# Layer 0's banded heads: from two score passes and a product by query to one pass, a softmax by query and weights turned by TensorE

## The chip, the cores and the metric

The kernel runs on one core of one Trainium2 chip. The metric is the device time of one execution in microseconds (us), taken as the median of several runs. An execution is also profiled once; all rows below come from that profile.

## What is computed

Two blocks follow each other: a two-layer attention block and a pool-and-feed-forward block. Layer 0 has eight global heads, eight banded ("window") heads and four memory heads, each gated and then projected out. Only the banded heads change. For each of the eight heads, 1024 queries stand in 8 blocks of 128, and each block sees its own and the two neighbouring blocks of keys:

```
def window_gqa(q, k, v, sink, rel_bias):
    ...
    rel = kpos[None, :] - qpos[:, None]
    band = jnp.abs(rel) <= WINDOW          # WINDOW = 128
    bias = rel_bias[t5_bucket(rel)]
    ...
        s = jnp.einsum('bqkgd,bskd->bkgqs', qblk, kb) * scale + bias
        s = jnp.where(valid, s, -jnp.inf)
        m = jnp.maximum(jnp.max(s, axis=-1, keepdims=True), sk)
        p = jnp.exp(s - m)
        denom = jnp.sum(p, axis=-1, keepdims=True) + jnp.exp(sk - m)
        return jnp.einsum('bkgqs,bskd->bqkgd', p / denom, vb)
```

`sk` is one learned number per head (the sink): it enters the maximum and the denominator, but has no value row.

## The kernel before, in words

All products are made of float32 numbers split into a high and a low part, so that one dense product is three matmuls (lines 261, 264 and 265: high by high, high by low, low by high).

Layer 0 runs two streams at once. `att` holds the attention of 12 items (four pairs of global heads, four pairs of banded heads, four memory heads). `fill` holds the dense products of layer 0: queries, keys, gates, and six of the eight column tiles of the output projection. `weave` lets each stream advance in proportion to numbers given by hand (232 for `att`, 290 for `fill`). A scheduler of the framework then sets the final order on each engine; `att` has the higher priority there, and the first of every four products of `fill` is tied behind an earlier score product of `att` (`mark` and `paced`). Every engine works through its list in order. All loads and stores are issued from SyncE's queue, also in order.

A banded pair `i` is done in two parts.

- `win_pre` (line 918 on), run beside the item before: for each head it multiplies each query block by its two or three key blocks (line 930, scores with the query in the partition), adds the bias and takes the maximum with the sink (line 931, in one VectorE instruction and a read of its accumulator). The eight columns of negated maxima are turned into rows (`max_row`, line 481) and written by DMA into the 65th row of the tile `W`.
- `win_main` and `pair_main`: the scores are multiplied a second time with the key in the partition (lines 557 and 558; the 65th row subtracts the maximum), the bias is added (line 955), then come the exponential (469), its high part (471) and its low part (142, half of them on GpSimd). `narrow` multiplies the weights of each query block by the values with the query in the partition (lines 668 and 669; the first two of 130 value columns are constants and give the denominator), closes a group of two or three query blocks with a copy, the sink, a reciprocal and two GpSimd instructions (679 to 685), and turns the finished blocks back (691).

The tiles of scores live in a pool of three PSUM buffers (`sp`, tag `s`), two more (`op`) hold the sums of the products with the values. `wide`, which the global heads use, has the values as weights and up to 512 queries as columns (lines 616 and 617).

Of the kernel before, what the change touches and what calls it, by code (L numbers as in the profile page):

```python
# [8 lines left out]
F32 = mybir.dt.float32  # L9
# [52 lines left out]

ROLL = [[0, 1, 2], [3, 4, 5], [6, 7]]
# [79 lines left out]
class Build:  # L145
# [377 lines left out]
    def v_tiles(self):  # L523

        V = [self.ap.tile([128, 8, 130], F32R, name=f"V{i}") for i in range(2)]
        for v in V:
            self.nc.gpsimd.memset(raw(v[:, :, 0:2]), 2.0)
        return V

    def load_v(self, v, V):  # L530

        for i in range(2):
            self.dma(out=V[:, :, 2 + 64 * i:66 + 64 * i], in_=v[i])

# [42 lines left out]
    def wide(self, O, U, V, tiles, perm=False):  # L577
# [30 lines left out]
        def pv(s, i, P):  # L608
            j, a, b = tiles[i]
            for g, x0, x1 in parts[i]:  # L610
# [5 lines left out]
                mm(o, V[s][:, j, 2:130], P[0][:, x], start=new, stop=False, skip_group_check=True)  # L616
                mm(o[0:64], V[s][:, j, 2:66], P[1][:, x], start=False, stop=i == touch[g][-1], skip_group_check=True)  # L617
# [3 lines left out]
        def close(s, g):  # L621
# [5 lines left out]
            if s == 0:  # L627
                return
# [15 lines left out]

    def narrow(self, O, U, V, tiles, groups, sink):


        nc = self.nc
        mm = nc.tensor.matmul
        group = {t: g for g, ts in enumerate(groups) for t in ts}  # L650
        touch = {}
        for i, (j, a, b) in enumerate(tiles):
            for t in range(a // 128, b // 128):
                touch.setdefault(group[t], []).append(i)
        bank = {}
        T = self.po.tile([128, 8, 2, 64], F32, tag="sg", name="T")

        def pv(s, i, P):
            j, a, b = tiles[i]
            with self.tc.manual_schedule(engines={mybir.EngineType.PE}):  # L660
                for t in range(a // 128, b // 128):
                    g = group[t]
                    new = (s, g) not in bank
                    if new:
                        bank[s, g] = self.op.tile([128, 512], F32, tag="od"[g % 2], name="o")[:, 0:130 * len(groups[g])].rearrange("p (t f) -> p t f", f=130)
                    x = slice(128 * t - a, 128 * t - a + 128)
                    o = bank[s, g][:, t - groups[g][0]]
                    mm(o, P[0][:, x], V[s][:, j], start=new, stop=False, skip_group_check=True)
                    mm(o[:, 0:66], P[1][:, x], V[s][:, j, 0:66], start=False, stop=i == touch[g][-1], skip_group_check=True)  # L669
            for g, ts in enumerate(groups):  # L670
                if i == touch[g][-1]:
                    close(s, g, ts)


        def close(s, g, ts):

            o, n = bank[s, g], len(ts)
            e = self.po.tile([128, 512], F32, tag="oe", name="oe", bufs=2)[:, 0:130 * n].rearrange("p (t f) -> p t f", f=130)
            (nc.scalar.copy if g % 2 else nc.vector.tensor_copy)(e, o)
            q = slice(ts[0], ts[-1] + 1)  # L680
            nc.vector.tensor_tensor(out=e[:, :, 0], in0=e[:, :, 0], in1=sink[s][:, q], op=ALU.add)
            R = self.small.tile([128, 8], F32, tag="R", name="R")
            nc.vector.reciprocal(R[:, 0:n], e[:, :, 0])
            nc.gpsimd.tensor_tensor(out=T[:, q, s], in0=e[:, :, 2:66], in1=e[:, :, 66:130], op=ALU.add)
            nc.gpsimd.tensor_tensor(out=T[:, q, s], in0=T[:, q, s], in1=R[:, 0:n].unsqueeze(2).to_broadcast([128, n, 64]), op=ALU.mult)
# [989 lines left out]
```

## Time and profile before

| | |
|---|---|
| median of 3 runs | 2456.99 us (2454.39 to 2458.63) |
| the profiled execution's own time | 2456.56 us |
| its span, first to last instruction | 2454.8 us |
| TensorE busy in the span | 2345.8 us (96%) |
| VectorE, ScalarE, GpSimd busy | 1733.0, 1069.4, 957.8 us |
| mean granted TensorE clock | 0.977 of full speed |
| banded heads, first to last instruction of their own | 471.5 to 734.8 us |

The table is read so: TensorE has work almost all the time, but its matmuls are pipelined and their ends modelled, so that a busy TensorE can still be slower than its best. Two things take time without showing as idle: a clock below 1, and short waits hidden under the modelled ends.

### The profile page before, as it was taken

The page shows a single profiled execution, that of the slowest core. Times are in us where ns is not written, and L with a number is a line of the kernel's source. Part 1 is how long each engine was busy: PE and PEld are TensorE (multiplying, and loading weights), DVE is VectorE, ACT ScalarE, POOL GpSimd, SP SyncE. Part 2 cuts the span into 40 slices and gives each one's busy share as a digit, 9 for nine tenths or more (in the row PEclk, how much of TensorE's full clock was granted, in tenths as well). Part 3 has the DMA queues.
Part 4 walks back from the last instruction along what each step waited for, and adds up shares of the span by engine and source line. Part 5 has one row for each costly group of instructions (what it writes and reads, how often), then busy time and mean ns, then how long its engine had stood idle before and what let it go on. Part 6 is the DMA issues. An engine that isn't in the chain of part 4 may idle for free.

```text
span 2454.8 us, 33066 instructions
## 1 busy us (share of the span) xinstructions
PE 2345.8 (96%) x11238; PEld 1927.1 (79%) x11238; DVE 1733.0 (71%) x2863; ACT 1069.4 (44%) x1937; POOL 957.8 (39%) x817
## 2 busy tenths in 40 slices
PE   7989999999999999999999999989899999999999
PEld 6966776777877878878897877867578888888887
DVE  6767987777776466777886889688977464646554
ACT  5425655564453364434453446444444131323231
POOL 3117886883340144547674772475600000000000
PEclk9989999998999999999999999999899999999999
DMA  6752234234455557676766656522122111111112
GB/s 207 215 144 65 86 106 122 91 102 137 125 195 198 188 189 194 173 214 186 206 167 195 184 172 239 165 86 78 62 77 79 48 52 43 52 48 48 48 48 90
DMA packets 235393, 314.37 MB, mean 128 GB/s; under 512 B 102007, under 2 KB 120951, under 8 KB 235224
## 3 DMA queue, kind: packets, MB, share of 16 engines
q1 hardware_dynamic: 235224, 312.26, 42.0%
q8 instruction: 89, 1.46, 0.3%
q14 instruction: 80, 0.66, 0.1%
HBM read 225.02 MB, written 87.03 MB: 127 GB/s over the span
## 4 chain that ended last, share of the span: by engine, by line
PE 76%; DVE 11%; DMA 5%; issue 3%; ACT 2%; POOL 2%; SPq 1%; DVEq 0%; POOLq 0%; ACTq 0%
PE ps L261 20%; PE ps L264 20%; PE ps L265 20%; PE s L557 3%; PE s L558 2%; DVE wlo L142 2%; PE o L617 2%; PE o L616 2%; DVE pl L142 1%; PE s L867 1%; PE s L1230 1%; DVE mcg L868 1%; DMA hl<-y 1%; DVE sx L1425 1%; POOL acc L606 1%
## 5 line engine op out<-in xcount | busy, mean ns | idle before, releaser
L261 PE MATMUL ps<-hh,whi 128*128 128x512 f32 x1888 | 749.0, 399 | 19.7 <-ACT hh L415 8.2
L264 PE MATMUL ps<-hl,whi 128*128 128x512 f32 x1888 | 751.6, 398 | 9.2 <-DVE hl L416 7.5
L265 PE MATMUL ps<-hh,wlo 128*128 128x512 f32 x1888 | 753.1, 399 | 3.6 <-DVE wlo L142 2.5
L242 ACT CAST whi<-wraw 128x512 fp32r<-128x512 f32 (+1 forms) x400 | 244.8, 614 | 481.4 <-PE ps L264 387.4
L261 PEld LDWEIGHTS ps<-hh,whi 128*128 128x128 f32 x1888 | 361.3, 192 | 98.8 <-ACT hh L415 8.2
L264 PEld LDWEIGHTS ps<-hl,whi 128*128 128x128 f32 x1888 | 361.4, 191 | 87.8 <-DVE hl L416 9.2
L265 PEld LDWEIGHTS ps<-hh,wlo 128*128 128x128 f32 x1888 | 361.1, 191 | 81.1 <-DVE wlo L142 3.7
L606 POOL TENSOR_TENSOR acc<-acc,p 128x512 f32<-128x512 f32 (+2 forms) x272 | 321.7, 1190 | 238.8 <-ACT p L469 185.7
L142 DVE TENSOR_TENSOR wlo<-wraw,whi 128x512 fp32r<-128x512 f32 (+1 forms) x388 | 327.6, 848 | 63.7 <-ACT whi L242 53.5
L142 POOL TENSOR_TENSOR pl<-p,ph 128x512 fp32r<-128x512 f32 (+2 forms) x192 | 234.1, 1222 | 79.2 <-ACT ph L471 66.9
L471 ACT CAST ph<-p 128x512 fp32r<-128x512 f32 (+2 forms) x304 | 162.2, 543 | 32.5 <-PE o L669 6.7
L469 ACT ACTIVATE p<-p 128x256 f32<-128x256 f32 (+2 forms) x192 | 98.1, 515 | 163.1 <-DVE p L1257 107.3
L1497 DVE TENSOR_TENSOR xacc<-ps,xacc 128x512 f32<-128x512 f32 x96 | 66.2, 691 | 131.4 <-PE ps L265 130.9
L1469 DVE TENSOR_TENSOR hz<-ps,rbc 128x512 f32<-128x512 f32 x88 | 60.7, 690 | 116.4 <-PE ps L265 114.1
L264 PE MATMUL ps<-al,whi 128*128 128x512 f32 x352 | 139.1, 396 | 0.0
L265 PE MATMUL ps<-ah,wlo 128*128 128x512 f32 x352 | 138.7, 396 | 0.0
L261 PE MATMUL ps<-ah,whi 128*128 128x512 f32 x352 | 138.4, 396 | 0.0
L1473 ACT ACTIVATE cv<-hz,vecs 128x512 f32<-128x512 f32 x88 | 71.6, 816 | 130.9 <-DVE hz L1469 128.4
L142 DVE TENSOR_TENSOR pl<-p,ph 128x512 fp32r<-128x512 f32 (+1 forms) x112 | 104.1, 929 | 28.6 <-ACT ph L471 21.4
L617 PE MATMUL o<-pl,V 128*64 128x384 f32 (+2 forms) x288 | 95.0, 348 | 9.9 <-DVE pl L142 6.4
L469 ACT ACTIVATE p<-s 128x512 f32<-128x512 f32 x112 | 66.3, 596 | 78.3 <-PE s L558 66.4
L1257 DVE TENSOR_TENSOR p<-s,MB 128x384 f32<-128x384 f32 (+2 forms) x128 | 68.8, 550 | 40.6 <-POOL pl L142 18.5
(259 smaller groups left out, 4478.7 us busy)
## 6 DMA issues: line engine op xcount, KB each, us to landing
wraw<-in_w SPq DMA_DIRECT2D x116, 256.0 KB
wraw<-in_wfi SPq DMA_DIRECT2D x112, 256.0 KB
wraw<-in_wo SPq DMA_DIRECT2D x72, 256.0 KB
g<-evf SPq DMA_DIRECT2D x48, 256.0 KB
wraw<-in_wfo SPq DMA_DIRECT2D x40, 256.0 KB
sg<-g SPq DMA_DIRECT2D x32, 256.0 KB
y<-O SPq DMA_DIRECT2D x14, 512.0 KB
hl<-y SPq DMA_DIRECT2D x14, 512.0 KB
```

The costliest lines, as they stand in the source:

```text
L142: out_eng.tensor_tensor(out=out, in0=a, in1=b, op=ALU.subtract)
L242: nc.scalar.copy(hi, raw[:, q:q + e])
L261: i = mm(ps, wh, h, start=first, stop=False, skip_group_check=True)
L264: mm(ps, wh, l, start=False, stop=False, skip_group_check=True)
L265: mm(ps, wl, h, start=False, stop=last, skip_group_check=True)
L469: nc.scalar.activation(p, s, AF.Exp)
L471: nc.scalar.copy(ph, p)
L557: self.mark(mm(ps[:, 0:n], K0[s][0:k0, js], U[s][0:k0, a:b], start=True, stop=False))
L606: nc.gpsimd.tensor_tensor(out=t, in0=t, in1=p[:, x0 - a:x1 - a], op=ALU.add)
L617: mm(o[0:64], V[s][:, j, 2:66], P[1][:, x], start=False, stop=i == touch[g][-1], skip_group_check=True)
L1257: nc.vector.tensor_tensor(out=p, in0=ps, in1=MB[:, s, o:o + b - a], op=ALU.add)
L1473: nc.scalar.activation(t, z[:, 2:514], AF.Identity, scale=self.v("cw2", j), bias=self.v("cb", j))
```

## The change

The first score pass, the second pass by key, the row of maxima and the product by query go away. One pass is left: the queries of the banded heads are stored negated (scale -0.125), the bias tile is negated once per pair on ScalarE, and the one VectorE instruction that was the first pass now gives the minimum, which is the negated maximum, over bias and negated sink (`nsink`). The exponential takes `scale=-1` and that minimum as its bias, and sums each row on the way. For every two query blocks the sink's share is added, a reciprocal taken, and the weights are multiplied by it and by 0.5 (one block on GpSimd, the other on VectorE). Then `turn` transposes, for each key block, its two or three pieces on TensorE into one PSUM tile of the same three-buffer pool; ScalarE copies the high part, VectorE makes the low part, and `wide` multiplies with the values. The values lose their two constant columns. `half` is now marked after the first head's scores, and for the fourth pair after the second head's last turn.

```
-        V = [self.ap.tile([128, 8, 130], F32R, name=f"V{i}") for i in range(2)]
+        return [self.ap.tile([128, 8, 128], F32R, name=f"V{i}") for i in range(2)]
...
-            if s == 0:
+            if s == 0 or not sums_to:
                 return
...
+    def load_uw(self, st, q, s):
+        U = self.load_hi(q, s)
+        W = self.up.tile([128, S], F32R, tag="W", name="W", bufs=2)
+        self.dma(out=W[0:64], in_=q[1][64 * s:64 * s + 64])
+        self.nc.gpsimd.memset(raw(W[64:65, :]), 0.0)
...
+                ps = self.sp.tile([128, 512], F32, tag="s", name="s")
+                self.mark(mm(ps[:, 0:n], U[:, ts], KA[:, ks], start=True, stop=False))
+                mm(ps[:, 0:n], W[0:65, ts], KB[:, ks], start=False, stop=True)
...
+                nc.vector.tensor_tensor_reduce(out=ps[:, 0:n], in0=ps[:, 0:n], in1=TA[:, s, o:o + n], scale=1.0, scalar=self.nsink[:, h:h + 1], op0=ALU.add, op1=ALU.min, accum_out=negm[:, bb])
+                nc.scalar.activation(p[:, 0:n], ps[:, 0:n], AF.Exp, scale=-1.0, bias=negm[:, bb], accum_out=D[:, bb])
...
+            nc.scalar.activation(es[:, mm2], negm[:, mm2], AF.Exp, bias=self.sink[:, h:h + 1])
+            nc.vector.tensor_tensor(out=es[:, mm2], in0=D[:, mm2], in1=es[:, mm2], op=ALU.add)
+            nc.vector.reciprocal(R[:, mm2], es[:, mm2])
...
+                (nc.gpsimd if n2 == 0 else nc.vector).tensor_scalar(out=P[s, b][:, 0:n], in0=P[s, b][:, 0:n], scalar1=R[:, b:b + 1], scalar2=0.5, op0=ALU.mult, op1=ALU.mult)
...
+        def turn(s, j):
+            _, a, b = tiles[j]
+            t = self.sp.tile([128, 512], F32, tag="s", name="pt")
+            for q in range(a // 128, b // 128):
+                o = (j - max(q - 1, 0)) * 128
+                nc.tensor.transpose(t[:, q * 128 - a:q * 128 - a + 128], P[s, q][:, o:o + 128], self.ident)
+            ph = self.pp.tile([128, b - a], F32R, tag="ph", name="ph")
+            nc.scalar.copy(ph, t[:, 0:b - a])
+            pl = self.pp.tile([128, b - a], F32R, tag="pl", name="pl")
+            sub(nc.vector, pl, t[:, 0:b - a], raw(ph))
...
+                new = [(s, j) for j in range(8) if (j <= 2 * m or m == 3) and (m == 0 or j > 2 * m - 2)]
+                ready += new
+                yield from behind(len(new), 1)
...
-                self.drain(weave((att(), 232.0), (fill, 290.0)))
+                self.drain(weave((att(), 245.0), (fill, 290.0)))
```

How this moves instructions is shown at three places. The first is TensorE in the middle of a banded pair before the change: `o` are sums of products with the values, `ph` and `pl` the high and low part of one tile of weights, `s` scores, `ps` a dense product of `fill`.

```order
L668 MATMUL o_6139<-V0_1626,ph_6151 128x130
L669 MATMUL o_6139<-V0_1626,pl_6153 128x66
L930 MATMUL s_6250<-KA1_1633,U_6067 128x256
L668 MATMUL o_6180<-V0_1626,ph_6151 128x130
L669 MATMUL o_6180<-V0_1626,pl_6153 128x66
L261 MATMUL ps_6386<-hh_83,whi_5830 128x512
L264 MATMUL ps_6386<-hl_84,whi_5830 128x512
L668 MATMUL o_6139<-V0_1626,ph_6170 128x130
```

There a tile of weights comes straight from the exponential of its scores, and the first pass of the next pair (line 930) stands between. The same engine, in the middle of the second banded pair after the change; `pt` are tiles of turned weights, `P` the weights by query:

```order
L915 MATMUL pt_5985<-ident_58,P_5864 128x128
L915 MATMUL pt_5985<-ident_58,P_5870 128x128
L915 MATMUL pt_5985<-ident_58,P_5888 128x128
L915 MATMUL pt_6001<-ident_58,P_5870 128x128
L915 MATMUL pt_6001<-ident_58,P_5888 128x128
L915 MATMUL pt_6001<-ident_58,P_5919 128x128
L609 MATMUL o_5935<-ph_5989,V0_1628 128x256
L609 MATMUL o_6011<-ph_5989,V0_1628 128x128
L895 MATMUL s_6018<-KA0_1631,U_5824 128x256
L896 MATMUL s_6018<-KB0_1630,W_5827 128x256
L257 MATMUL ps_6137<-hh_83,whi_5906 128x512
```

The high part `ph_5989` is ScalarE's copy of `pt_5985`; its first product now stands three transposes behind the last transpose that it needs, and the next scores and the dense products are queued behind it.

The second place is the start of the second banded pair on TensorE, after the change:

```order
L895 MATMUL s_5861<-KA0_1631,U_5488 128x384
L896 MATMUL s_5861<-KB0_1630,W_5491 128x384
L895 MATMUL s_5867<-KA0_1631,U_5488 128x384
L896 MATMUL s_5867<-KB0_1630,W_5491 128x384
L915 MATMUL pt_5878<-ident_58,P_5838 128x128
L895 MATMUL s_5885<-KA0_1631,U_5488 128x384
L896 MATMUL s_5885<-KB0_1630,W_5491 128x384
L915 MATMUL pt_5878<-ident_58,P_5853 128x128
L895 MATMUL s_5916<-KA0_1631,U_5488 128x384
L896 MATMUL s_5916<-KB0_1630,W_5491 128x384
L257 MATMUL ps_6024<-hh_83,whi_5636 128x512
```

`P_5838` and `P_5853` are the weights of the first two query blocks of this pair, whose scores stand only a few rows earlier; no dense product lies between.

The third place is VectorE in the same pair. Before the change, in a banded pair's main part (`oe` is a closed group of products, `mt` the row of maxima):

```order
L955 TENSOR_TENSOR p_6352<-s_6349,TB_6056 128x384
L142 TENSOR_TENSOR pl_6307<-p_6302,ph_6305 128x256
L955 TENSOR_TENSOR p_6370<-s_6367,TB_6056 128x384
L142 TENSOR_TENSOR pl_6357<-p_6352,ph_6355 128x384
L483 CAST mt_6401<-s_6399 8x128
L679 COPY oe_6342<-o_6245 128x260
L931 ISA s_6407,mc_6406<-s_6407,TA_6064,sink_1624 128x256
```

After it, where the transposes of the first place are copied (`evl` and `wlo` belong to `fill`):

```order
L426 SCALAR_TENSOR_TENSOR evl_6095<-evf_6092,evh_6094 128x512
L138 TENSOR_TENSOR pl_5991<-pt_5985,ph_5989 128x384
L138 TENSOR_TENSOR pl_6007<-pt_6001,ph_6005 128x384
L903 TENSOR_TENSOR es0_5833<-mc_5832,es0_5833 128x2
L898 ISA s_6018,negm_6014<-s_6018,TA_5341,nsink_1626 128x256
L898 ISA negm_6014 128x1
L904 RECIPROCAL R_5834<-es0_5833 128x2
L908 TENSOR_SCALAR P_5977<-P_5977,R_5834 128x256
```

Every low part is now VectorE's, and the small instructions of the softmax stand in line between the large ones.

## Rows read from the trace of the kernel before

**Rows 1.** The page's first line.

```profile
span 2454.8 us, 33066 instructions
```

**Rows 2.** Busy time by stage: stretch, length, PE, PEld, DVE, ACT, POOL (instructions), granted clock, DMA.

```profile
541.00:735.00 194.00, 180.74 (x978) 154.69 (x976) 150.71 (x361) 97.34 (x217) 82.33 (x95) 0.93 0.49 155
735.00:926.00 191.00, 185.07 (x893) 152.18 (x892) 101.05 (x163) 80.90 (x137) 35.19 (x32) 0.99 0.59 193
140.00:541.00 401.00, 377.76 (x1580) 287.84 (x1579) 315.41 (x433) 215.94 (x377) 296.10 (x204) 0.96 0.32 95
```

**Rows 3.** The same view in steps of 5 us within the banded heads.

```profile
560.00:565.00 5.00, 3.69 (x17) 3.69 (x17) 5.00 (x11) 1.96 (x4) 1.29 (x3) 0.65 0.28 105
565.00:570.00 5.00, 4.90 (x20) 4.20 (x19) 4.93 (x21) 0.68 (x2) 3.01 (x4) 0.50 0.40 157
...
595.00:600.00 5.00, 3.84 (x21) 3.24 (x20) 3.91 (x11) 2.87 (x7) 2.48 (x4) 1.00 0.37 134
```

**Rows 4.** Groups of TensorE instructions by form, 460 to 740 us.

```profile
L668 PE MATMUL o<-V,ph 128*128 128x130 f32 x176 | 45.1, 302 | 1.6 <-ACT ph L471 0.9 <-DVE oe L679 0.6
L669 PE MATMUL o<-V,pl 128*128 128x66 f32 x176 | 41.4, 248 | 3.0 <-POOL pl L142 1.6 <-DVE pl L142 1.4
...
L930 PE MATMUL s<-KA,U 128*128 128x384 f32 x48 | 17.3, 397 | 1.4 <-DVE mc L931 1.1
...
L930 PE MATMUL s<-KA,U 128*128 128x256 f32 x16 | 5.4, 337 | 1.2 <-DVE oe L681 1.1
```

**Rows 5.** TensorE's instructions in order of time: start, length, instruction.

```profile
606.19 0.66 PE L691 MATMUL ot<-ident,T 128*128 128x128 f32 x4
606.60 0.42 PE L930 MATMUL s<-KA,U 128*128 128x384 f32 x1
...
625.76 0.28 PE L930 MATMUL s<-KA,U 128*128 128x256 f32 x1
625.88 0.34 PE L557 MATMUL s<-U,KA 128*128 128x384 f32 x1
626.05 0.34 PE L558 MATMUL s<-W,KB 65*128 65x384 f32 x1
626.23 0.40 PE L261 MATMUL ps<-hh,whi 128*128 128x512 f32 x1
626.47 0.40 PE L264 MATMUL ps<-hl,whi 128*128 128x512 f32 x1
...
629.49 0.31 PE L668 MATMUL o<-V,ph 128*128 128x130 f32 x1
...
629.71 0.31 PE L668 MATMUL o<-V,ph 128*128 128x130 f32 x1
```

**Rows 6.** Groups of VectorE instructions by form, 460 to 740 us.

```profile
L931 DVE CUSTOM_DVE_ANT_0 s<-s,TA,sink 128x384 f32<-128x384 f32 x48 | 28.7, 618 | 5.0 <-PE s L930 4.7
L955 DVE TENSOR_TENSOR p<-s,TB 128x384 f32<-128x384 f32 x48 | 26.2, 550 | 2.8 <-POOL pl L142 0.8 <-PE s L558 0.7
...
L931 DVE DVE_READ_ACCUMULATOR2_ANT mc<- 128x1 f32 x64 | 8.8, 138 | 0.0
...
L955 DVE TENSOR_TENSOR p<-s,TB 128x256 f32<-128x256 f32 x16 | 6.5, 416 | 7.4 <-DMA TB<-in_winB 6.4 <-POOL pl L142 0.9
```

**Rows 7.** What TensorE waited for, 460 to 740 us: total, times, longest.

```profile
PE s L557 <- DVE mc L931: 2.8, 3, 2.2
...
PE s L557 <- DVE p L955: 1.7, 2, 1.2
...
PE s L930 <- DVE mc L931: 1.1, 3, 0.7
PE s L930 <- DVE oe L681: 1.1, 1, 1.1
```

**Rows 8.** Groups of ScalarE instructions by form, 460 to 740 us.

```profile
L469 ACT ACTIVATE p<-p 128x384 f32<-128x384 f32 x48 | 25.0, 524 | 34.4 <-DVE p L955 34.0 <-DVE r L725 0.4
L471 ACT CAST ph<-p 128x384 fp32r<-128x384 f32 x48 | 24.1, 509 | 5.9 <-PE o L669 3.3 <-PE o L668 1.0 <-PE d L635 0.8
```

**Rows 9.** The same view for GpSimd.

```profile
L142 POOL TENSOR_TENSOR pl<-p,ph 128x384 fp32r<-128x384 f32 x24 | 25.3, 1053 | 50.0 <-ACT ph L471 38.0 <-PE s L930 11.9
```

More of the change, by code (lines that the diff above doesn't have):

```diff
@@ L643, in wide @@
         return dest, take, pv, back
[L645 to L685, printed above, removed]
-        def back(c, sg):
-            ps = self.rq.tile([128, 512], F32, tag="r", name="ot")
-            for t in range(4):
-                nc.tensor.transpose(ps[:, t * 128:(t + 1) * 128], T[:, 4 * c + t].rearrange("p s d -> p (s d)"), self.ident)
-            nc.vector.tensor_tensor(out=O[:, 512 * c:512 * c + 512], in0=ps, in1=sg, op=ALU.mult)
-        return None, lambda s, i, p: None, pv, back
@@ L912, in win_pre @@
[L912 removed]
+        TA = st["TA"] = self.bp.tile([128, 2, 384], F32, tag=f"t{i % 2}", name="TA")
         for s in range(2):
             self.dma(out=TA[:, s, :], in_=self.A["winA"][2 * i + s])
[L915 to L941 removed]
@@ L943, in win_main @@
+        self.nc.scalar.activation(TA, TA, AF.Copy, scale=-1.0)
+        yield from after(self.done, ("half", st["n"] - 1))
+        st["UW"] = []
+        self.load_uw(st, self.qb[i], 0)
+        yield 0.1
     def win_main(self, st, i):
         nc = self.nc
+        mm = nc.tensor.matmul
         self.phase = "win"
-        self.load_W(st, self.qb[i])
-        TB = self.bp.tile([128, 2, 384], F32, tag="t1", name="TB")
-        for s in range(2):
-            self.dma(out=TB[:, s, :], in_=self.A["winB"][2 * i + s])
@@ L950, in win_main @@
-        yield from self.wait(T_LOAD)
-        tiles = [(j, max(j - 1, 0) * 128, min(j + 2, 8) * 128) for j in range(8)]
-        def bias(p, ps, s, j, a, b):
-            o = a - (j - 1) * 128
-            nc.vector.tensor_tensor(out=p, in0=ps, in1=TB[:, s, o:o + b - a], op=ALU.add)
-        yield from self.pair_main(st, self.prods0(st), [st["K"][2]] * 2, tiles, partial(self.narrow, groups=ROLL, sink=st["es"]), bias)
+        self.load_uw(st, self.qb[i], 1)
+        KB, KA, V = st["K"]
+        TA = st["TA"]
@@ new lines, in behind @@
+        def behind(keep, left):
+            while len(ready) > keep:
+                turn(*ready.pop(0))
+                yield 0.33
+                if len(turned) > left:
+                    pv(*turned.pop(0))
+                    yield 0.35
+        steps = {}
+        for s in range(2):
+            for m in range(4):
+                yield from softmax(s, m, steps)
+                if m == 3 and s == 0 and i < 3:
+                    self.done.add(("half", st["n"]))
+                new = [(s, j) for j in range(8) if (j <= 2 * m or m == 3) and (m == 0 or j > 2 * m - 2)]
+                ready += new
+                yield from behind(len(new), 1)
@@ L957, in win_main @@
+        yield from behind(0, 1)
+        self.done.add(("half", st["n"]))
+        while turned:
+            pv(*turned.pop(0))
         yield from after(self.done, ("g", 4 + i))
@@ L1059, in layer0 @@
             kb = T(1, self.plain_evac(*self.kb, 1.0), "kb")
[L1060 removed]
+            qb = [T(6 + i, self.plain_evac(*self.qb[i], -0.125), "qb", i) for i in range(4)]
             qm = [T(10 + i, self.plain_evac(*self.qm[i], 128.0 ** -0.5), "qm", i) for i in range(4)]
@@ L1094, in layer0 @@
             self.dma(out=self.sink, in_=A["sink"])
+            self.nsink = self.ap.tile([128, 8], F32, name="nsink")
+            nc.vector.tensor_scalar(out=self.nsink, in0=self.sink, scalar1=-1.0, scalar2=None, op0=ALU.mult)
             Vt = self.v_tiles()
```

70 lines of the change are left out of this document (28 added, 42 removed).

## The prediction

> **What bounds the kernel now.** I read the busy shares first, then the granted clock, by stage and by 5 us, then the groups of TensorE and VectorE instructions where the banded heads run, then TensorE's instructions in order of time, and last what TensorE waited for. The stage of the banded heads, from the last global scores to the last turned block, is 541 to 735 us [rows 2]. TensorE is busy in 180.7 of its 194 us, VectorE in 150.7, ScalarE in 97.3, GpSimd in 82.3. So TensorE bounds it, with 13.3 us of idle time, and VectorE, at 78%, stands close behind. A second loss is the clock: its mean there is 0.93, so about 0.07 x 194 = 13.6 us of full-speed time are missing. The 5 us rows show where it goes: after 1.3 us of idle in one stretch the next runs at 0.50, the lower of the two levels (1.2 GHz), with TensorE busy in 4.90 of 5 us; yet 595 to 600 us has as much idle time and a clock of 1.00 [rows 3]. Gaps on TensorE can thus cost more than their length, but don't always.
>
> **Prices.** TensorE's busy times can't be added, because ends are modelled: a 384-column product lasts 0.34 us, but the next starts 0.17 us later. I take start-to-start distances [rows 5]: 0.12 us for 256 columns, 0.17 for 384, 0.24 for 512, 0.22 for a pair of lines 668 and 669, and 0.41 for four transposes, so 0.10 each.
>
> *Removed from TensorE:* the first score pass, 48 x 0.17 + 16 x 0.12 = 10.1 us; the products by query, 176 pairs x 0.22 = 38.7 us [rows 4]; 32 back-transposes, 3.2 us. Sum 52.0. The 8 small transposes of maxima I leave out.
>
> *Added:* per head 8 key blocks have 22 query blocks in them, so 176 transposes, 17.6 us. The products with the values: two of the eight blocks are cut at column 512, so per head there are four pieces of 384 columns, four of 256 and two of 128, each for high and low. That is 64 x 0.17 + 64 x 0.12 + 32 x 0.10 (a value between nothing and the 256-column price) = 21.8 us. Sum 39.4. The scores that stay are the same shapes and number, only with sides swapped. **Net on TensorE: -12.6 us.**
>
> The weakest price is the transpose. Nothing shows one below 0.10, but at half of it the sum is 8.8 us lower. The last of the four ends 0.25 us after the next instruction has started, so one that overlapped nothing would take 0.35, and 176 of them 61.6 us, 44 more. I take 0.10, since in the new order they stand in threes, close to the row.
>
> The Trainium skill (TensorE: Matmul & The Clock Gate, Part 4: PE-mode transpose) gives about 275 ns for a transpose within a kernel, as a length; by that figure as a price 176 would be estimated at 48 us and the change would lose 18 us on TensorE. The row speaks against using it so: each of the four started 0.10 us after the one before.
>
> *VectorE.* Removed: 64 bias additions, 26.2 + 6.5 = 32.7 us [rows 6], 32 low parts, the group closes, the casts of maxima. Added: 64 low parts that read PSUM, for which the bias addition is the nearest row (same shapes, one operand in PSUM), so 32.7 us again; 32 scalings at no more than 0.55 each, 17.6; 64 instructions of one or two columns; 16 closing additions. The 64 minima cost what the maxima cost (0.618 + 0.138). I call it even: VectorE isn't relieved, and must do its 150 us in a stage that should shrink.
>
> *Costed at nothing.* ScalarE gains 64 reads of row sums (the nearest, VectorE's read, 0.14), and 36 copies, exponentials and negations of at most 0.52 [rows 8]: 28 us on an engine idle in 97. GpSimd loses 32 low parts of about 1.05 [rows 9] and the closes, and gains 32 scalings, bounded by the same 1.05, and 8 rows of zeros; if one of these were late, a head's scores would wait about 1 us, 8 in all. Sixteen DMAs go (second bias tile, rows of maxima). The fourth pair lets the memory heads start later; the dense products of the output projection cover that, and without the cover the idle time of the last stage, 191.0 - 185.1 = 6 us [rows 2], might double. The scheduler's other shifts: counted in the two orders, 888 instead of 941 of the 1728 dense 512-column products of `fill` stand before the last global score. Those 53 x 0.24 = 12.7 us move into later stages. The sum is unchanged as long as the global stage is TensorE's, busy in 377.8 of 401 us; GpSimd, in 296.1, is the other candidate, and were the stage its own, up to 12.7 us would come back as loss.
>
> **The waits that take each other's place.** Going: TensorE's waits for the first pass and for the late second bias tile, 2.8 + 1.7 + 1.1 + 1.1 = 6.7 us [rows 7]. Coming: three chains, each with a floor without queues.
> 1. Last transpose to the high product: 0.25 (its tail) + 0.51 (copy) = 0.76 us. I counted TensorE's work between them in the new order, at the prices above: 14 of 64 turns have less than that, short by 4.3 us in all.
> 2. Last transpose to the low product: 0.76 + 0.55 = 1.31; 15 of 64 are short, by 5.5 us.
> 3. Scores to their transpose: 0.16 (tail) + 2 x 0.756 (both minima) + 0.52 + 1.05 = 3.25; 2 of 64 are short, by 3.6 us. Both stand at the start of the second pair, with nothing of `fill` between.
>
> Sum 13.4 us. A wait for the high part shortens the one for the low part, which takes something off; VectorE's queue (low parts behind minima, scalings and `fill`'s evacuations) puts something on. I leave it at 13.4. What is queued behind such a wait are the next scores and the dense products, since TensorE works in order; and the next scores hold up VectorE. **Net: +6.7 us.** Lower bound: the old waits go and nothing comes, -6.7; upper bound below, under the rivals.
>
> **Sum.** -12.6 + 6.7 = -5.9 us against the profiled execution's own 2456.56 us (its span is 2454.8 [rows 1], 1.8 us lie around it), which is 0.4 below the median. **Forecast: 2450.7 us**, with 2445 to 2455 for this case alone. A change under 0.2% (4.9 us) is about what can't be told from none.
>
> **Rivals.**
> - *The clock falls more often (slower).* New gaps of 0.5 to 4 us, spread over the whole stage, let the granted clock drop as in 565 to 570 us. For: every one of 32 steps (two query blocks) gets short waits where the old order had them only around a change of pairs. Against: 595 to 600 us, a gap without a drop. Place: 541 to 735 us. Price: a mean of 0.85 in place of 0.93 costs 15.5 us, so 2466; 0.80 costs 25, so 2476. It decides from a clock of about 0.87 on, where its 10.8 us eat the 5.9 and the 4.9 of the bound. The Trainium skill says in the same section that transposes don't count as busy for the clock gate. By that the added 176 would speak for this rival; the rows here don't settle it.
> - *VectorE and the three PSUM buffers set the pace (no change).* Four tiles per step now pass through three buffers; before also four, but a score tile was free after one VectorE instruction (0.62 or 0.55), and now waits for the exponential too (0.52), a turned tile for copy and low part (0.51 + 0.55). For: VectorE's 78%. Against: its time falls to no engine that is already full. If each step loses 0.2 us more, 32 x 0.2 = 6.4 us, nothing is left: 2457.
> - *The gain shows in full (clearly faster).* The old waits go, ScalarE and VectorE are always ahead: -12.6 - 6.7 = -19.3, so 2437. Against: the floors, which need no queue.
> - *The work by query costs more than assumed (slower)*, transposes at 0.20: +17.6, so 2468. The row of four speaks against it.
>
> **Chances.** Forecast 0.40; no change by VectorE 0.20; the clock 0.23; full gain 0.12; dear transposes 0.05. The forecast's own spread reaches across the 0.2% bound, so 0.28 of its 0.40 count as faster and 0.12 as same; of the VectorE case 0.02 are faster, 0.14 same, 0.04 slower. Faster 0.42, same 0.26, slower 0.32. The range that leaves out no more than 2 in 10 is 2434 (full gain, with cheaper transposes in part) to 2474 (clock near 0.81).
>
> **What would show it.** Right: transposes about 0.1 us apart; in the stage of the banded heads a TensorE that waits for ScalarE's `ph` and VectorE's `pl` and `P`, together 10 to 20 us; VectorE's busy time near 150 us in a stage a few us shorter; the stage of global heads some 10 us shorter, the one after the banded heads some 10 us longer. Wrong on the slow side: a granted clock under 0.87 in the stage, or VectorE without gaps. Wrong on the fast side: TensorE's idle time there at or below the old 13 us. A difference in layer 1 or later would be one that I haven't seen: the scheduler orders some of its instructions anew.

## The result and the profile after

The changed kernel takes 2475.59 us (median of 4, 2474.55 to 2477.95), the kernel before 2456.21 (2454.39 to 2458.63) in the same runs: a ratio of 1.0076, with a 95% interval of 1.0062 to 1.0091. It is 19 us slower. The forecast was 2450.7 us, with 2434 to 2474 as its range.

The profile of the changed kernel, its span and busy times:

```profile
span 2473.1 us, 32804 instructions
...
PE 2344.1 (95%) x11118; PEld 1910.2 (77%) x11118; DVE 1728.3 (70%) x2856; ACT 1091.8 (44%) x2037; POOL 925.9 (37%) x773
```

The same three stages as in [rows 2], cut at the last global score, the last turned block and the first score of layer 1 (columns as there; in [rows 2] the order is banded, behind, global):

```profile
140.00:540.20 400.20, 369.18 (x1517) 277.46 (x1516) 304.10 (x393) 214.58 (x374) 294.11 (x204) 0.95 0.30 91
540.20:733.50 193.30, 169.24 (x841) 135.72 (x839) 140.74 (x360) 106.48 (x283) 44.20 (x51) 0.95 0.44 134
733.50:943.20 209.70, 200.50 (x979) 164.68 (x977) 121.67 (x198) 95.09 (x174) 41.03 (x35) 0.98 0.60 199
```

Three things are to be seen. The global heads' stage has less work for TensorE (369.2 us busy, not 377.8) and lasts as long as before: 400.2 and 401. The banded stage has much less (169.2 for 180.7) and also lasts as long: 193.3 and 194; TensorE's idle time there went from 13.3 to 24.1 us. And the stretch behind is 18.2 us longer. So both stages ahead gave nothing back for the work that they lost, and the work that was pushed out of them was paid behind: of the 18.2 us there 15.4 are more work for TensorE (200.5 us busy, 185.1 before) and 2.8 more idle time. Layer 1 and the rest take 1530 us in both.

The work that was pushed out is of two kinds. The first is the memory heads' products, the ones that read the tile `mkv`. Before:

```profile
541.00:735.00 194.00, 7.32 (x42) 5.72 (x42) 0.93 0.49 155
735.00:926.50 191.50, 22.31 (x102) 16.56 (x102) 0.99 0.59 193
```

After:

```profile
733.50:943.20 209.70, 29.40 (x144) 23.12 (x144) 0.98 0.60 199
```

All 42 that stood in the banded stage now stand behind it, 7.1 us of TensorE's busy time. So 7.3 of the 11.5 us that the banded stage lost are theirs, and not a saving of the banded heads.

The second kind is dense products, here in counts of the one line that stands for a third of `fill` (line 261 before, 257 after; it has a few products of other kinds too), in the same stretches. Before:

```profile
140.00:541.00 401.00, 110.56 (x275) 53.43 (x275) 0.96 0.32 95
541.00:735.00 194.00, 47.88 (x115) 23.29 (x115) 0.93 0.49 155
735.00:926.50 191.50, 97.22 (x252) 47.62 (x252) 0.99 0.59 193
```

After:

```profile
140.00:540.20 400.20, 103.23 (x259) 49.87 (x258) 0.95 0.30 91
540.20:733.50 193.30, 51.11 (x123) 24.74 (x123) 0.95 0.44 134
733.50:943.20 209.70, 101.08 (x262) 49.16 (x262) 0.98 0.60 199
```

16 products of this line, 48 with its two sisters, 11 us at 0.23 us each, left the stage of the global heads. That stage kept its length because TensorE's idle time in it rose from 23.2 to 31.0 us and because its granted clock fell from 0.96 to 0.95, by estimate some 4 us of 400.

What TensorE waited for in the banded stage of the changed kernel (total us, times, longest), all of it:

```profile
PE s L895 <- DVE pl L138: 4.8, 10, 0.9
PE o L609 <- ACT ph L917: 4.3, 7, 1.2
PE pt L915 <- POOL P L908: 4.3, 3, 3.3
PE s L895 <- ACT P L899: 3.4, 7, 0.9
PE o L610 <- DVE pl L138: 3.2, 7, 0.7
PE d L629 <- POOL al L138: 1.7, 1, 1.7
PE pt L915 <- ACT P L899: 0.9, 1, 0.9
PE o L610 <- POOL pl L138: 0.5, 1, 0.5
PE pt L915 <- DVE pl L138: 0.2, 1, 0.2
```

The prediction's three chains are the second, third, fifth and seventh of these: 4.3 + 4.3 + 3.2 + 0.9 = 12.7 us, where it had 13.4. New is what stands before line 895: 8.2 us, 17 times, on VectorE's low part or ScalarE's exponential. The scores read neither. They write into a PSUM buffer, and it is still held by an older tile. One such place, in order of time:

```profile
616.44 0.86 ACT L917 CAST ph<-pt 128x384 fp32r<-128x384 f32 x2
...
617.38 0.48 ACT L899 ACTIVATE P<-s,negm 128x256 f32<-128x256 f32 x1
...
617.74 0.21 ACT L899 ACTIVATION_READ_ACCUMULATOR P<-s,negm 128x1 f32 x1
...
618.00 0.39 PE L895 MATMUL s<-KA,U 128*128 128x256 f32 x1 [0.59 <-ACT P L899]
...
618.35 0.39 PE L257 MATMUL ps<-hh,whi 128*128 128x512 f32 x1
```

ScalarE copies two high parts first, then takes an exponential and reads its sum, until 617.95; only then can the next score start, and the dense products are queued behind it.

### The profile page after: what moved, and what is told of

The parts are those of the page before. It is cut to its first block, busy times and chain, and to the rows that moved or that the text cites. A ratio compares the mean times of both kernels' runs of the same rounds, so it can differ in the third digit from the quotient of the medians.

```text
span 2473.1 us, 32804 instructions
## 1 busy us (share of the span) xinstructions
PE 2344.1 (95%) x11118; PEld 1910.2 (77%) x11118; DVE 1728.3 (70%) x2856; ACT 1091.8 (44%) x2037; POOL 925.9 (37%) x773
## 4 chain that ended last, share of the span: by engine, by line
PE 70%; DVE 13%; DMA 5%; issue 4%; ACT 3%; POOL 3%; SPq 1%; DVEq 0%; ACTq 0%; POOLq 0%
PE ps L257 19%; PE ps L260 19%; PE ps L261 19%; DVE wlo L138 2%; PE s L550 2%; POOL acc L599 2%; PE o L610 2%; PE s L551 2%; PE o L609 1%; DVE pl L138 1%; DVE mcg L811 1%; PE s L1218 1%; POOL pl L138 1%; PE s L810 1%; SPq L158 1%
## 5 line engine op out<-in xcount | busy, mean ns | idle before, releaser
L138 POOL TENSOR_TENSOR pl<-p,ph 128x384 fp32r<-128x384 f32 (+1 forms) x160 | 199.6, 1250 | 7.2 <-ACT ph L467 7.0
L610 PE MATMUL o<-pl,V 128*64 128x512 f32 (+3 forms) x368 | 121.8, 348 | 22.3 <-DVE pl L138 14.4
L467 ACT CAST ph<-p 128x512 fp32r<-128x512 f32 (+1 forms) x240 | 132.2, 560 | 18.9 <-POOL al L138 5.2
L609 PE MATMUL o<-ph,V 128*128 128x512 f32 (+3 forms) x368 | 120.7, 346 | 4.4 <-ACT ph L917 4.3
L465 ACT ACTIVATE p<-p 128x384 f32<-128x384 f32 (+2 forms) x128 | 66.6, 524 | 110.5 <-DVE p L1245 110.1
```

Of the source, the lines that this page charges most:

```text
L138: out_eng.tensor_tensor(out=out, in0=a, in1=b, op=ALU.subtract)
L465: nc.scalar.activation(p, s, AF.Exp)
L467: nc.scalar.copy(ph, p)
L609: mm(o, V[s][:, j, :], P[0][:, x], start=new, stop=False, skip_group_check=True)
L610: mm(o[0:64], V[s][:, j, 0:64], P[1][:, x], start=False, stop=i == touch[g][-1], skip_group_check=True)
```

## The experiments

Each time stands beside runs of the kernel before on the same chip (medians 2456.2 to 2459.0). The runs were made on several chips; where two of them are compared in us, the ratios, each against its own chip, are the safer measure. Stage lengths are those of the one profiled execution. Layer 1 and the rest, which no edit touches, took between 1524.5 and 1535.6 us in these profiles, so a single span is good to some 5 us, and the stages say more.

| run | us | ratio to before, interval | global ends | banded | behind |
|---|---|---|---|---|---|
| before | 2456.2 | 1 | 541.2 | 193.2 | 192.1 |
| changed | 2475.6 | 1.0076 (1.0062 to 1.0091) | 539.8 | 192.8 | 210.5 |
| a232 | 2464.8 | 1.0025 (1.0013 to 1.0036) | 540.6 | 197.8 | 197.5 |
| ascaled | 2472.9 | 1.0060 (1.0041 to 1.0078) | 538.9 | 187.1 | 219.0 |
| b245 | 2474.9 | 1.0075 (1.0054 to 1.0096) | 543.2 | 195.9 | 202.6 |
| alate | 2471.4 | 1.0055 (1.0040 to 1.0070) | 538.2 | 191.4 | 211.1 |
| c1 | 2467.0 | 1.0047 (1.0029 to 1.0065) | 536.3 | 194.8 | 196.5 |
| c2 | 2448.4 | 0.9954 (0.9936 to 0.9972) | 540.9 | 178.9 | 196.0 |
| c215 | 2443.5 | 0.9939 (0.9921 to 0.9957) | 540.2 | 179.4 | 193.9 |
| bhalf | 2454.5 | 0.9987 (0.9975 to 0.9999) | 537.7 | 186.1 | 190.8 |
| arq | 2453.9 | 0.9973 (0.9959 to 0.9986) | 538.4 | 178.8 | 201.9 |
| b220 | 2460.8 | 1.0002 (0.9988 to 1.0016) | 547.6 | 197.2 | 183.7 |
| c200 | 2459.1 | 1.0001 (0.9988 to 1.0015) | 562.3 | 168.4 | 195.0 |
| c215l | 2446.2 | 0.9954 (0.9936 to 0.9972) | 541.4 | 179.7 | 194.1 |
| asfree | 2461.0 | 1.0013 (1.0002 to 1.0024) | 539.5 | 184.9 | 204.3 |
| c215s | 2439.6 | 0.9912 (0.9895 to 0.9929) | 542.0 | 174.3 | 194.1 |
| b4 | 2481.8 | 1.0081 (1.0053 to 1.0110) | 541.5 | 221.2 | 187.5 |

The theory at the start (A): the weave number, 245 for 232, took dense products out of a stage that lasts 400 us anyway (below, the thin weave). Rivals: that stage is TensorE's after all (B), or the loss sits in the chains of the banded heads (C).

**a232**

```
-                self.drain(weave((att(), 245.0), (fill, 290.0)))
+                self.drain(weave((att(), 232.0), (fill, 290.0)))
```

> The changed kernel with the old weave number, 232 for 245; nothing else. By the order of instructions 924 instead of 888 dense 512-column products then stand before the last global score (before the change: 941), 366 instead of 367 between it and the last turned block, 630 instead of 665 behind. Theory A (the stage of the global heads is not TensorE's: it lasts 400 us with 777 such products or with 824, so products taken out of it come back as a loss later): the stage stays at 400 to 402 us, the banded stage at 193, and 35 products x 0.23 = 8 us go from the stretch behind: 2467.5 us. Rival B (the stage of the global heads is TensorE's): it grows by the 8 us, and the time stays at 2475.6. Rival C (the loss sits in the chains of the banded heads alone): as B, no change.

Measured 2464.8, 10.8 us less than the changed kernel. The stage of the global heads ends at 540.6, with 270 products of line 257 in place of 259: theory A. The other 6.6 us to the kernel before on the same chip (2458.2) are still open here.

**ascaled**

```
-                yield 0.37
+                yield 0.28
-                yield 0.33
+                yield 0.25
-                    yield 0.35
+                    yield 0.27
```

with 232 as in a232: the costs of a block of scores, of a turn and of its products.

> The changed kernel with the old weave number 232 and the three costs that the banded heads report to the weave cut to 0.28, 0.25 and 0.27, so that both streams stand to each other as before the change. 924 dense products before the last global score, 312 (not 366) in the banded stage, 684 (not 630) behind it: 54 products = 12.4 us moved out of the banded stage. Theory A for the banded stage as well (its length is set by the chain of the heads, not by TensorE): it stays at 193 us and the 12.4 us come back behind it, 2480. Rival B (TensorE sets the banded stage): it shrinks by 12 us, and the time is that of the kernel with 232 alone, about 2467.

2472.9. Neither fits alone: the banded stage does shrink, by 10.7 us against a232, with 12.4 us less work in it, but the stretch behind grows by 21.5. Of these 15.9 are TensorE's busy time (206.4 us, 190.6 in a232), the moved products at a clock of 0.98 where a232 had 1.00, and 5.6 are idle time (12.5 us, 6.9 in a232). So the length of the banded stage isn't fixed as the global stage's is.

**b245**

```
-                self.drain(weave((att(), 232.0), (fill, 290.0)))
+                self.drain(weave((att(), 245.0), (fill, 290.0)))
```

(in the kernel before)

> The kernel before the change with the new weave number, 245 for 232; nothing else. 900 instead of 941 dense products before the last global score, 360 instead of 340 in the banded stage, 660 instead of 639 behind. Theory A: the stage of the global heads stays at 401 us with 9.4 us less work for TensorE, and at least the 21 products behind (4.8 us) are lost, 2461; 2466 if the banded stage was TensorE's before and takes its 20 more in full. Rival B or C: no change, 2456.

2474.9: this one number makes the old kernel as slow as the changed one. Its global stage ends at 543.2 with 263 products in place of 275. The loss is larger than theory A gave (5 to 10 us): the stretch behind takes 10.5 us more for 21 products, 4.8 us. In the trace TensorE is idle there for 11.0 us, 6.4 before; 4.3 of them it waits for the keys of the memory heads (2.5 before), and its clock is 0.97 in place of 0.99, by estimate some 4 us of 203. So the rest is idle time and clock; why both came is not shown.

**alate**

```
-        self.nc.scalar.activation(TA, TA, AF.Copy, scale=-1.0)
         yield from after(self.done, ("half", st["n"] - 1))
         st["UW"] = []
         self.load_uw(st, self.qb[i], 0)
+        self.nc.scalar.activation(TA, TA, AF.Copy, scale=-1.0)
```

> The changed kernel, weave number as changed, with ScalarE's negation of the bias tile placed behind the wait for the first half of the pair before, instead of right behind the tile's two loads. In the changed kernel ScalarE waits twice for these loads, 6.6 us in all, with the high copies of turned tiles queued behind it. Theory C (chains through ScalarE and VectorE pace the banded stage): the stage loses 3 to 6.6 us, 2469 to 2472.5. Theory A alone (the banded stage has other slack): no change, 2475.6.

2471.4, 4.2 us less, as theory C had it, but the intervals overlap, and only 1.4 us of it show in the banded stage.

**c1** (a232 and alate together)

> The changed kernel with both single edits so far: weave number 232, and the bias tile's negation behind the wait for the first half of the pair before. The two had given 10.8 us (2464.8) and 4.2 us (2471.4). If they take away different waits, they add up: 2460.6 us, and the banded stage is 4 us shorter than with 232 alone (197.8). If the denser dense products hide ScalarE's wait for the bias tile: 2464.8.

2467.0: they don't add. With 232 the negation's place is worth nothing that can be measured.

**c2** (c1 and a fourth buffer)

```
-            t = self.sp.tile([128, 512], F32, tag="s", name="pt")
+            t = (self.rq if j % 2 else self.sp).tile([128, 512], F32, tag="r" if j % 2 else "s", name="pt")
```

> As c1 (232, negation behind the wait), and every second turned tile goes to the PSUM buffer that the square sums and row broadcasts of the global heads use, so that scores and turned tiles have four buffers in place of three. Theory: three buffers pace the scores (TensorE waits 8.2 us for ScalarE's exponential or VectorE's low part before line 895, where a score tile takes the buffer of an older tile); with four most of it goes: 4 to 8 us less than c1, 2453 to 2457. Rival: the buffers aren't the limit, the same waits move to the next product of the chain: the time of c1.

2448.4: 18.6 us less, more than twice what was expected, and 0.5% faster than the kernel before, with an interval that lies below 1. The banded stage falls from 194.8 to 178.9 us. The place is not the one that was expected. In c1 TensorE waits only 3.1 us before line 895, where the changed kernel has 8.2; its long waits there are those for the low and the high part:

```profile
PE o L610 <- DVE pl L138: 9.0, 13, 1.9
PE o L609 <- ACT ph L917: 6.6, 8, 3.7
```

and in c2:

```profile
PE o L609 <- ACT ph L917: 3.8, 3, 1.5
...
PE o L610 <- DVE pl L138: 2.5, 3, 1.7
```

So where the lack of a buffer shows in the list of waits depends on how many dense products stand between; with 232 the fourth buffer shortens these two, by 9.3 us.

**c215** (c2 with 215)

> As c2, and the weave number 215: 984 dense products before the last global score (c2: 924), 306 in the banded stage (366), the same behind. 60 products = 13.8 us move forward. If the stage of the global heads still had room (400 us with TensorE busy in 377), it stays near 401 and the banded stage shortens by 11 to 14 us: 10 us less than c2. If TensorE now sets it, it grows by as much as the banded stage shrinks: the time of c2. Something between, by the share that is still free, is likeliest: about 5 us less than c2.

2443.5. By the orders 20 triples of products moved forward, and neither the global stage (400.2 us, now with 290 products of line 257) nor the banded one changed its length. The 4.9 us lie within the two intervals. The clock is part of why: in the banded stage it falls from 0.94 (c2) to 0.90, and 60 products less leave TensorE only 3 us less busy (158.8 for 161.9); in the global stage it rises from 0.96 to 0.98.

**bhalf** (the kernel before)

```
-            if s == 0:
+            if s == 0 and not (self.phase == "win" and st["n"] == 7):
                 self.done.add(("half", st.get("n")))
+        self.done.add(("half", st.get("n")))
```

> The kernel before the change, with the fourth banded pair's `half` marked at the end of its second head instead of after the first, as in the changed kernel; so the memory heads start as late as there. By the order 5 dense products and 2.9 us of TensorE's work move from the banded stage behind it. If the late start of the memory heads is covered, as the prediction had it: no change, 2456 to 2458. If it is a cost of its own: up to 6 us, 2463.

2454.5, no loss. But the edit doesn't bring about the late start that it was to test: in its trace 36 of the memory heads' products still stand in the banded stage, where the kernel before has 42 and the changed kernel none. What their late start costs in the changed kernel is not shown by this run, nor by another.

**arq** (the changed kernel, 245, with the one line of c2)

> The changed kernel, weave number as changed (245), with one edit: every second turned tile in the fourth PSUM buffer. With 232 and the late negation this edit gave 18.6 us (2467.0 to 2448.4), all of it in the banded stage (194.8 to 178.9 us). Theory: the three buffers pace the banded stage whatever the weave number: 15 to 18 us less than the changed kernel, 2457 to 2461. Rival: the gain needs the denser weave, since with 245 the loss sits in the stage of the global heads and behind: 2470 or more.

2453.9, 21.7 us less than the changed kernel: the fourth buffer alone makes it faster than the kernel before, with the thin weave as it is. By the ratios, 1.0076 to 0.9973, it is 25 us. What TensorE waited for in its banded stage:

```profile
PE o L610 <- DVE pl L138: 2.7, 4, 1.1
PE pt L915 <- DVE pl L138: 1.9, 2, 1.7
PE pt L915 <- POOL P L908: 1.7, 3, 0.8
...
PE o L609 <- ACT ph L917: 1.7, 2, 1.1
PE pt L915 <- ACT P L899: 1.6, 2, 1.0
PE s L895 <- ACT P L899: 1.5, 4, 0.5
...
PE s L895 <- DVE pl L138: 0.2, 1, 0.2
```

Before line 895 the 8.2 us are 1.7 now. The stage in one row:

```profile
538.40:717.20 178.80, 163.56 (x867) 135.89 (x865) 143.46 (x371) 109.83 (x295) 50.82 (x53) 0.97 0.51 158
```

The same dense products (124 of line 257, 123 before) pass in 14.5 us less. The stretch behind takes 201.8 us in place of 209.7. In the two stretches together TensorE is idle for 11 us less (22.3, 33.3 in the changed kernel), and the clock is 0.97 and 1.00 in place of 0.95 and 0.98, by estimate some 8 us more; so about a third of the gain comes by way of the clock.

**b220** (the kernel before with 220) and **c200** (c215 with 200)

> The kernel before the change with weave number 220: 984 dense products before the last global score, 306 in the banded stage, 630 behind, the same three counts as the changed kernel with four buffers and 215 (2443.5 us). If the stage of the global heads has room for 43 more products in this kernel too, the gain of the denser weave belongs to neither version of the heads, and the kernel before falls to about 2450. If 232 is its best, 2456 to 2462. The comparison with 2443.5 then is the banded heads' change alone, at equal density: my sum for TensorE gives 12.6 us, so 2456.

> The changed kernel with four buffers, late negation and weave number 200: 1056 dense products before the last global score (215: 984), 234 in the banded stage (306). 72 products = 16.6 us move forward once more. If the stage of the global heads (540 us at its end with 984 and TensorE's work by counts at 455.7 us) still has room: 5 us less than with 215, 2438. If it is now TensorE's, it grows by up to 16 us, and the banded stage, whose own chain needs some 150 us, shrinks by less: 2445 to 2455.

b220: 2460.8, no change, though it has the same counts of dense products in the three stages as c215. The difference of the two, 17 us (15 by the ratios), is the change of the banded heads at equal density and with enough buffers, the late negation included, and with what comes by the clock (0.87 in b220's banded stage, 0.90 in c215's) and by the memory heads (the stretch behind is 10 us longer in c215). c200: 2459.1, the move too far. Its global stage, in all and in the count of line 257, first c215's:

```profile
140.00:540.20 400.20, 380.36 (x1606) 289.88 (x1604) 314.94 (x404) 217.97 (x378) 291.15 (x202) 0.98 0.31 97
140.00:540.20 400.20, 115.68 (x290) 55.55 (x289) 0.98 0.31 97
```

and c200's, the count alone:

```profile
140.00:562.30 422.30, 126.59 (x316) 60.88 (x315) 0.96 0.32 98
```

With 259, 270 and 290 products of line 257 the stage takes 400 us; 26 more (78 with the sisters, 18 us) cost 22. So up to 290 the stage has room for them, beyond that it hasn't. Of the room from 259 to 290 one half was idle time of TensorE (31.0 us, then 19.8) and the other came by the clock (0.95, then 0.98, some 12 us of 400). In the old heads the room ends sooner: in b220, with 291, the stage takes 7 us more than in the kernel before. What else sets the 400 us was not tried; GpSimd is busy in 294 of them.

**c215l** (c215, two turned tiles kept back)

```
-                yield from behind(len(new), 1)
-        yield from behind(0, 1)
+                yield from behind(len(new), 2)
+        yield from behind(0, 2)
```

> As the changed kernel with four buffers, late negation and 215, but with two turned tiles kept behind the products instead of one, so that each product with the values stands one turn later. TensorE still waited there for ScalarE's high copy 3.5 us and for VectorE's low part 3.3 us. If that is on the path: 3 to 6 us less, 2438 to 2440. If the later product holds the tile of values' sums or the high and low parts longer, and the next copy waits for them: no change, 2443.

2446.2: no gain. But the edit hardly touched the waits that it was aimed at: 3.0 us for the high part and 3.3 for the low (c215: 3.5 and 3.3). So whether they are on the path is not shown.

**asfree** (the changed kernel, 245, three buffers), after which what holds the buffers was to be told apart:

```
-                nc.vector.tensor_tensor_reduce(out=ps[:, 0:n], in0=ps[:, 0:n], ...)
-                nc.scalar.activation(p[:, 0:n], ps[:, 0:n], AF.Exp, ...)
+                nc.vector.tensor_tensor_reduce(out=p[:, 0:n], in0=ps[:, 0:n], ...)
+                nc.scalar.activation(p[:, 0:n], p[:, 0:n], AF.Exp, ...)
```

> The changed kernel, weave number 245 and three buffers as changed; VectorE's minimum instruction writes its sums to the weights' tile in SBUF instead of in place, and the exponential reads them there. So a score tile's buffer is free after one VectorE instruction (0.62 us), as before the change, and no longer waits for ScalarE (0.58 us and its queue). If the score tiles hold the buffers too long: most of the 21.7 us that the fourth buffer gave, 2455 to 2462. If the turned tiles hold them: 0 to 5 us, 2470 to 2476.

2461.0: 14.6 of the 21.7 us (by the ratios 15 of 25). So some two thirds come with the score tile that no longer waits for the exponential; that the rest is the turned tile is argued, not shown. A second rival stands beside the buffers: each of these edits also lets the scheduler order the stage anew. Of the 758 products of lines 895, 896, 915, 609 and 610 among TensorE's first 4500 instructions, 708 stand in the same sequence in asfree as in the changed kernel, and 647 in arq. How much of either gain is the buffer itself and how much the order that it allows, no run separates. The exponential isn't faster from SBUF (610 ns, from PSUM 576). How the heads' scores are spread over time, by line 895 (shortest, median, longest ns; first and last start) in the changed kernel:

```profile
L895 PE MATMUL s<-KA,U x64: 277/386/669, 540.2 to 725.5; 128*128 128x384 f32 x48, 128*128 128x256 f32 x16
```

in asfree:

```profile
L895 PE MATMUL s<-KA,U x64: 277/376/667, 539.9 to 714.2; 128*128 128x384 f32 x48, 128*128 128x256 f32 x16
```

and in arq:

```profile
L895 PE MATMUL s<-KA,U x64: 274/339/689, 538.8 to 702.6; 128*128 128x384 f32 x48, 128*128 128x256 f32 x16
```

From first to last 185.3, 174.3 and 163.8 us: per step of two query blocks (32 steps) 0.34 and 0.67 us less. What TensorE still waits for before line 895 in asfree:

```profile
PE s L895 <- DVE pl L138: 5.8, 11, 1.2
...
PE s L895 <- DVE negm L898: 1.9, 4, 0.8
```

ScalarE's exponential is gone from the list, VectorE's minimum stands there instead, and the low parts of turned tiles are still the longest. The visible waits before line 895 fell only from 8.2 to 7.7 us, so the list of waits doesn't show most of what the held buffer costs; the clock does in part (0.97 in the stage and 1.00 behind it, as in arq).

**c215s** (c215 and asfree together)

> The changed kernel with four buffers, late negation, 215 and the minimum written to SBUF. If both edits take away the same wait: the time without the last, 2443.5. If four buffers were still short of one: 2438 to 2441.

2439.6, 0.9912 of the kernel before (0.9895 to 0.9929): the lowest median of all. It can't be told from c215: the intervals of c215 and c215s overlap by 8 in 10,000.

**b4** (the kernel before with a fourth buffer)

```
-                ps = self.sp.tile([128, 512], F32, tag="s", name="s")
+                q = bias is not None and self.phase == "win" and i % 2
+                ps = (self.rq if q else self.sp).tile([128, 512], F32, tag="r" if q else "s", name="s")
```

> The kernel before the change with every second score tile of the banded heads' second pass in the fourth buffer, weave number 232. If the fourth buffer is worth something only because the change holds tiles longer: no change, 2456 to 2460. If the kernel before was short of buffers too: 5 to 10 us less, 2450.

2481.8, slower, and neither expectation. TensorE's longest waits in its banded stage:

```profile
PE s L558 <- DVE p L956: 10.1, 10, 3.0
...
PE s L558 <- DVE O L693: 3.3, 3, 1.9
```

The scores now wait for the bias addition and for the turned blocks that use the same buffer there. So the old kernel had no lack that this edit cures; another way to give it a buffer wasn't tried.

## Why the prediction was wrong

- **TensorE's work, -12.6 us: right.** Six transposes in a row take 0.57 us (0.095 each) in these rows of the changed kernel, and the pieces of 384 columns follow each other in 0.17:

```profile
611.13 0.82 PE L915 MATMUL pt<-ident,P 128*128 128x128 f32 x6
611.70 0.42 PE L895 MATMUL s<-KA,U 128*128 128x384 f32 x1
...
614.93 0.33 PE L609 MATMUL o<-ph,V 128*128 128x384 f32 x1
615.10 0.34 PE L610 MATMUL o<-pl,V 128*64 128x384 f32 x1
615.27 0.28 PE L895 MATMUL s<-KA,U 128*128 128x256 f32 x1
```

  The rival of dear transposes falls. At equal density and with four buffers the change is worth 15 to 17 us (c215 against b220). That is near the 12.6, but it holds the clock, the late negation and the old waits too, so it doesn't measure TensorE's work alone.
- **Three chains, +13.4 us: right in size**, 12.7 measured in the list of waits. Chain by chain it is in part luck: 4.3 us for the high part as forecast, 3.2 for the low where it had 5.5, and 5.2 for the weights where it had 3.6. The wait of 3.3 us at the start of the second pair is there, and the clock falls behind it, as in [rows 3]:

```profile
600.00:605.00 5.00, 1.59 (x7) 1.27 (x8) 4.24 (x15) 3.21 (x11) 1.11 (x2) 0.85 0.31 108
605.00:610.00 5.00, 5.00 (x14) 4.09 (x14) 3.17 (x10) 1.90 (x6) 0.81 (x2) 0.50 0.26 105
```

- **The three PSUM buffers: the step that failed most.** The prediction had the mechanism only as a rival, in the right words (a score tile waits for the exponential too, a turned tile for copy and low part), with an assumed 0.2 us per step, 6.4 us in all. The fourth buffer shortens a step by 0.67 us and gives 21.7 us. The 0.2 came from no row. A floor without queues, as the prediction used for its chains, would not have given the right one either. A score tile's minimum and exponential with their two reads take 0.615 + 0.136 + 0.576 + 0.193 = 1.52 us in the changed kernel, a turned tile's copy and low part 0.479 + 0.550 = 1.03; two of each through three buffers is 1.7 us by estimate, in a step of 5.8 (185.3 us by 32). By this it is the queues in front of these instructions that fill the buffers, which is argued and not measured. VectorE isn't full, at 140.7 of 193.3 us, but its low part ends 10 of the 17 waits before line 895. The Trainium skill (Perfetto Trace Analysis, Identifying Performance Opportunities, Optimization Strategy) says that the same gap repeating on the engine that should be full can mean that SBUF or PSUM has no room for the next tile. The changed kernel's trace agrees: 17 waits before line 895, the longest 0.9 us, and 1.7 us in all with a fourth buffer.
- **The dense products moved out of the global stage, costed at nothing: wrong.** The condition was written down ("as long as the global stage is TensorE's") with its price if false, 12.7 us, and taken as true from a busy share of 94%. In the changed kernel it was false: the stage takes 400 us with 259 or 290 products of a line. Going back to 232 gives 10.8 us with three buffers (12.5 by the ratios); the thin weave alone costs the old kernel 0.75% (b245), some 18. This term and the buffers overlap: each alone (a232, arq) gives back 10.8 and 21.7 us, together with the late negation (c2) 27.2, not 32.5.
- **The clock: not as that rival had it.** Its mean in the banded stage is 0.95, before 0.93 [rows 2]. It isn't neutral, though: the shortfall from 1.00, summed over the three stages, goes from some 31 to some 34 us, and several of the edits above give or take a part of their time by way of it.
- **The memory heads' late start, costed at nothing: open.** All 42 of their products that stood in the banded stage moved behind it, where they take 7.1 us of TensorE, and the banded stage kept its length. bhalf moved only 6 of the 42 and doesn't settle it.
- **VectorE's own sum: as costed.** Over the three stages it is busy for 567 us before and after; the 10 us less in the banded stage stand behind it. ScalarE's sums were read in 0.193 us each, not 0.14, and its exponential from PSUM took 0.576, not 0.52; both lengthen the hold of a score tile.

The sum with the measured terms, each from its own run and so only rough: -12.6 - 6.7 + 12.7 + 21.7 + 10.8 is +26, against +19 measured; the last two overlap by 5, and the fourth buffer also takes 5 of the 12.7 us (7.7 are left in arq). What stays open: what sets the global stage's 400 us beside the clock, what the memory heads' late start costs, and how the buffers' gain divides between the hold itself and the order that the scheduler makes of it.

## What to carry to other kernels

When a change lengthens the time that a tile holds a shared PSUM buffer, look at the queues in front of the engines that empty it, and not only at the lengths of their instructions, which would have shown no lack here. A spare buffer is quickly tried: here one line that used another pool's buffer turned a loss of 19 us into a small gain (0.9973), and an earlier release of the score tile gave some two thirds of the gain. A busy share of 94% doesn't say that a stage is TensorE's: take some of its filler work out or put more in, and see whether its length moves, before work that moves between stages is costed at nothing. A number that balances two streams has to be set anew whenever the cost of one of them changes, and tried alone in the kernel before, so that its loss isn't charged to the change. And before a run is read as a test, its trace should show that the edit did what it was made for: bhalf and c215l didn't.

## What was unexpected in the hardware's behaviour

GpSimd scaled 128x384 weights in 0.717 us, where the low part of the same shape had taken 1.053 [rows 9]. Busy share doesn't tell whether the global stage has room for more: in c215 TensorE is busy in 380.4 of 400.2 us (95%) and the stage keeps the length that it has with less work; in b220 in 384.5 of 407.7 (94%), and it is already 7 us longer than in the kernel before; in c200 in 403.7 of 422.3 (96%). And with more dense products in that stage its granted clock was higher, 0.95, 0.96 and 0.98 with 259, 275 and 290 of the counted line; with 316, in c200, it was 0.96.
